# Spacing the first layer's attention steps in a woven program, charging gate loads to its issue clock, fetching gate rows ahead, and a later place for the first layer's block sums

## The chip, the core and the metric

The kernel runs on one core of a Trainium2 chip. Its time is device microseconds of that core, as the median of several runs. Five engines work side by side: TensorE (PE in the profile; PEld is its weight load), VectorE (DVE), ScalarE (ACT), GpSimd (POOL), and SyncE (SP), which here only issues DMAs. Each engine runs its own instructions in program order and waits on semaphores for the others.

## What is computed

Two layers of a trunk over 512 latent and 256 context tokens, 1024 channels wide. The reference, cut to what matters:

```python
for l in range(DEPTH):                       # DEPTH = 2
    sh, sc, gt = split(silu(c) @ w_ada[l] + b_ada[l])        # for latents; the same from c_ctx for the context
    h = rmsnorm(x, g_pre[l]) * (1 + sc) + sh
    p = split(h @ w_in[l])                   # columns for: conv, attention, GLA, SiLU paths, merge gates
    att = softmax_attention(q, k, v)         # 8 query heads, 2 key/value heads, rotary on latents
    gla = bidirectional_gla(q, k, v, decay)  # 4 heads, chunked linear attention
    br_a = (conv mixer * silu(z)) @ w_br_conv[l]
    br_b = (att * silu(z_attn)) @ w_br_attn[l]
    br_c = (rmsnorm(gla, g) * silu(z_gla)) @ w_br_gla[l]
    out = (g_a * br_a + g_b * br_b + g_c * br_c) @ w_out[l]
    x = x + gt * rmsnorm(out, g_post[l])     # the context stream too, in the first layer
```

## The kernel before

Every product is made in three passes of float32 parts: an operand is split into a high part (ACT copies, line 143) and a low part (DVE subtracts, line 134). Most DVE work goes through one helper, `tt` at line 134, so tiles and not lines tell its instructions apart.

The program is a hand-made list of steps. A `Step` (line 76) holds a function that emits instructions, the weight units it needs, a `cost` (its PE time in ns as the author counts it), and a `lat`, the latency that should lie in front of it. `weave(main, side)` (line 85) lays a list of dependent steps (side) into a list of independent products (main): it adds up `cost * room` over main, divides by the sum of `lat` over side, and lets each side step come as soon as main steps worth its `lat` times that scale have been placed.

In the first layer there are two weaves. The first (line 1634) lays `mods_next` into main: the next layer's modulation (`small_vectors`, two `ada_half`) and this layer's gate rows (`gate_rows`, line 507). The second (line 1640) lays attention and then the four GLA heads (`side = att + sum(heads, [])`) into main. Main there is, in this order: one convolution block, then 34 pairs of projections (`pair_steps`, line 335, seven steps p1 to p7 each; a pair shares work between two column blocks by sums of blocks), then the products of the convolution branch (`w_br_conv`) and of the attention branch (`w_br_attn`), four steps a column block. The 64 branch steps have `room = 1.7`, which makes them count for more main than they cost. Eight empty steps of cost 1500 and eight of 2500 (`behind`, line 1215) stand between them for loads of branch inputs; they bring no PE work.

The latencies come from a table; the first number of each pair is the first layer's:

```python
"kv_ctx": (2400, 1500), "kv": (1500, 1200), "k_rope": (1000, 2000), "k_rot": (2500, 2500), "k_tr": (4000, 4000),
"q_ctx": (2400, 1500), "q": (1500, 1500), "q_rope": (2500, 2500), "q_rot": (2500, 2500), "q_tr0": (5000, 5000),
"q_tr1": (1500, 1950), "values": (500, 500), "weights": (3000, 3000), "scores": (1000, 1500),
"g_r": (1920, 2400), "g_q": (1500, 1500), "g_parts": (0, 0), "g_decays": (1000, 1000), "g_k": (1500, 1500),
"g_decays2": (0, 300), "g_v": (1500, 1500), "g_v2": (1500, 1500), "g_diag": (1500, 1500), "g_lev0": (2500, 2500),
"g_lev": (5500, 5500), "g_fin": (1500, 562), "g_ktr": (5000, 5000), "g_qfin": (0, 800), "g_st0": (3000, 3000),
"g_st1": (1000, 500), "g_st2": (1000, 1600), "g_outtr": (1000, 1000), "g_scaled": (1000, 1000),
"g_outs": (1500, 1500),
```

Attention (line 566) has, for each of 2 key/value heads and 2 pairs of query heads, projections into PSUM, norms and rotation on ACT and DVE, transposes, and then six rounds of three steps: `scores` (line 699: PE at line 708 into the tile psA, maxima on DVE, exponentials on ACT), `weights` (line 723: normalisation on DVE at lines 752 and 753, transposes on PE at line 158 into psA, a split by ACT and DVE into pThi and pTlo) and `values` (PE, line 761). psA has two buffers, which scores, weights, the larger bursts of projections, and GLA share.

A GLA head (line 783) has projections q, k and v (`side_cols`, `v_burst`), `decays` (line 833), a `diagonal` and seven `level` steps (line 940: products on PE at line 899, then on DVE two merges into a, two products into Q, two into K, one masked copy into att, and two products on POOL), then `finals`, transposes (`key_tr`), `states` (line 975), `outs` (line 996), `scaled` (line 1012) and `out_tr` (line 1025).

`gate_rows(l)` computes the gate as eight small products into the tile `mod`, then one last step (line 509): for each of two rows (b_ada, to be added, and g_post, to be multiplied) it clears a tile gp on POOL, loads the row into it by two DMAs on SP, and applies it to `mod` on DVE, all in one step.

Ahead of the first weave, at the start of the first layer, the input is normalised, transposed and modulated in four quarters of two blocks of 128 channels (`first_h`, line 1523). Each quarter has four steps: `scaled` (DVE scales and shifts into x0T, ACT writes the high part of hT), `sums` (DVE forms sums and differences of blocks into t, which only the pairs need; not in the last quarter), `low` (DVE writes the low part of hT, which every product needs) and `parts` (ACT and DVE split t into tx). Lines 1612 to 1614 write out their order between the modulation's quarters and the steps C, X and Z of the first convolution block, whose matmuls (line 238, tiles psA<-hT,hl) read hT quarter by quarter.

The list is walked once at build time (lines 1691 to 1749) with an issue clock that adds up the steps' costs. `advance` decides at each step which weight unit is loaded next (if a buffer of its ring is free) and which is split next: not before the issue clock has passed the unit's assumed arrival, `dma + LOAD_NS`, where `dma` adds up the time of each unit loaded. Other loads, such as those of stored gates `sg` and of partial sums `m` in the branches (lines 1266, 1269 and 1327), do not enter `dma`.

Of the kernel before, what the change touches and what calls it, by code (L numbers as in the profile page):

```python
# [17 lines left out]
P = 128  # L18
D = 1024
# [81 lines left out]
def trunk(ctx, tc, T, out):  # L101
# [16 lines left out]
    def L(dt=F32, name="l"):  # L118
        return pool.tile([P, 512], dt, tag="L", bufs=3, name=name)
# [9 lines left out]

    mm, act, dve, pl = nc.tensor.matmul, nc.scalar, nc.vector, nc.gpsimd  # L130
    load = nc.sync.dma_start

    def tt(o, a, b, op, e=dve):
        e.tensor_tensor(out=o, in0=a, in1=b, op=op)  # L134
# [371 lines left out]

    def gate_rows(l):

        def fn():
            for src, op in ((T["b_ada"][l][2 * D:], ALU.add), (T["g_post"][l], ALU.mult)):  # L510
                t = L(name="gp")[64:128, :512]
                pl.memset(t, 0.0)
                for j in range(2):
                    load(out=t[32 * j:32 * j + 2, :], in_=src[j * 512:(j + 1) * 512].partition_broadcast(2))
                tt(mod[64:128, :], mod[64:128, :], t, op)

        return ada_rows(l, (2 * D, 2 * D + 512), (64,)) + [Step(fn, lat=3)]

    def gate_broadcast(gb, t, j):
        pb = psB()  # L520
# [724 lines left out]
    def branch(l, nq, br, wname, Y, vec, mg_dram, sg_d=None):  # L1245

        def src_y(kb, c):
            return [t[:, c] for t in Y[kb]]

        S = []  # L1250
        for nb in range(NK):
            c = {}
            rows = slice(nb * P, (nb + 1) * P)
            tile_of = M if sg_d is None else G

            def evac_g(ps, st, c=c, nb=nb):
                c["sg"] = M(name="sg")
                act.activation(out=c["sg"][:, :nq], in_=ps[0][1], func=AF.Sigmoid,
                               bias=vec["v"][:, V_GATE + br * 8 + nb:V_GATE + br * 8 + nb + 1])
                if br == 0:  # L1260
                    exp_table()

            def before(st, c=c, rows=rows, tile_of=tile_of):
                if sg_d is not None:
                    c["sg"] = M(name="sg")
                    load(out=c["sg"], in_=sg_d[rows, :])
                if br > 0:
                    st["m"] = tile_of(name="m")
                    load(out=st["m"][:, :nq], in_=mg_dram[br - 1][rows, :nq])

            def evac_y(ps, st, c=c, rows=rows):
                sg = c["sg"]
                for x, p in ps:
                    tt(sg[:, x], sg[:, x], p, ALU.mult)
                if br > 0:
                    tt(sg[:, :nq], sg[:, :nq], st["m"][:, :nq], ALU.add)
                later.append(lambda: load(out=mg_dram[br][rows, :nq], in_=sg[:, :nq]))

            if sg_d is None:
                S += col_steps(unit_a(T["w_in"][l], O_MG + br * D + nb * P), src_h, nq, evac_g)  # L1280
            S += col_steps(unit_a(T[wname][l], nb * P), src_y, nq, evac_y, before)
        return S

    def branch_c(l, nq, u_dram, vec, mg_dram, merged, sz, sg_d=None, z_d=None):
# [36 lines left out]
        for nb in range(NK):  # L1321
            def before(st, nb=nb):
                st["m"] = (M if z_d is None else G)(name="m")
                pl.dma_start(out=st["m"][:, :nq], in_=mg_dram[1][nb * P:(nb + 1) * P, :nq])
                if sg_d is not None:
                    sg[nb] = G(name="sg")
                    load(out=sg[nb], in_=sg_d[nb * P:(nb + 1) * P, :])

            def evac_y(ps, st, nb=nb):
                t = sg[nb]  # L1330
                for x, p in ps:
                    tt(t[:, x], t[:, x], p, ALU.mult)
                tt(st["m"][:, :nq], t[:, :nq], st["m"][:, :nq], ALU.add)
                merged.append(split_to(st["m"][:, :nq], nq))

            rest += col_steps(unit_a(T["w_br_gla"][l], nb * P), src_y, nq, evac_y, before)
# [254 lines left out]
    for l in range(DEPTH):  # L1591
# [15 lines left out]
        if l == 0:  # L1607
# [1 line left out]
            (q0, f0), (q1, f1), (q2, f2), (q3, f3) = quarters  # L1609
            split = lambda u: Step(lambda: None, u[0].units)  # L1610
            ctx_loads[-1].opens = C[0].units
            prog += q0 + [Step(lambda kb=kb: raw_h(kb)) for kb in range(4, NK)] + [f0] + h0[0][:1] + [split(C)] + h0[0][1:]
            prog += [C[0], split(X)] + q1 + [X[0], split(Z), f1] + h0[1] + [Z[0], C[1]] + q2 + [X[1], f2] + h0[2] + [Z[1], C[2]]
            prog += q3 + [X[2], f3] + h0[3] + [sv[1], Z[2], C[3], X[3], Z[3]]
            prog += [Step(lambda: set_masks(0, 4)), Step(lambda: set_masks(4, 7))]
        else:
            hs = lagged(h_steps(0, range(NK), vec))
# [10 lines left out]
        if l == 0:  # L1628
# [7 lines left out]
                s.cost = max(s.cost, 1.0)  # L1636
            for s in main[main.index(first[-32]):]:
                s.room = 1.7
            side = att + sum(heads, [])
            woven = weave(main, side)  # L1640

# [47 lines left out]
        return n  # L1689

    clock, settled, ends = 0.0, 0, []
    dma = 0.0

    def finish(u):

        if u.rest:
# [7 lines left out]

    def advance(i, needed):

        nonlocal n_load, n_prep, settled, dma
        for u in units[:n_load]:
            if u.rest and clock >= u.done + REST_NS:
                finish(u)  # L1710
# [4 lines left out]
        while moved:  # L1715
            moved = False
            if n_load < len(units) and live(i, units[n_load].ring) < AHEAD[units[n_load].ring] and i >= hold.get(id(units[n_load]), 0):
                u = units[n_load]
                u.load(u)
                dma = max(dma, clock) + u.ns  # L1720
                u.arrival = dma + LOAD_NS
                n_load += 1
                moved = True
            if n_prep < len(line) and line[n_prep] in units[:n_load]:
# [74 lines left out]
```

## Time and profile before

| | us |
|---|---|
| median of 3 runs | 2536.9 (2532.49, 2536.9, 2538.5) |
| the profiled execution's own time | 2529.78 |
| its span, first to last instruction | 2528.0 |
| DVE busy | 1493.9 (59%) |
| ACT busy | 976.7 (39%) |
| POOL busy | 306.6 (12%) |

The times in all that follows are microseconds from the start of the span. In a view of stretches, each row gives a stretch, its length, the busy time of PE, PEld, DVE, ACT and POOL in it with the number of instructions, the share of its clock that TensorE was granted, the busy share of the DMA engines and their GB/s. In a view of groups, a row gives line, engine, operation, tiles out<-in, shapes and count, then the busy time, the mean duration in ns, and the engine's idle time just before those instructions with what ended it. In the view of instructions in order of time, a row gives start, duration, engine, line, operation, tiles, count, and in brackets the idle time before it with what ended it.

In the first layer, attention's steps run from about 97 to 726 us and GLA's from 726 to 1364 us; the pairs of projections end near 1047 us, where the branch products begin. The layer's output product follows, and the second layer runs from about 1510 us.

### The profile page before, as it was taken

What the parts mean: (1) busy time and instruction counts of PE and PEld (TensorE: products, weight loads), DVE (VectorE), ACT (ScalarE), POOL (GpSimd) and SP (SyncE); (2) the same over time, 40 slices, a digit from 0 to 9 for tenths busy, and PEclk for the clock granted to TensorE, in tenths of its full rate; (3) what the DMA queues carried; (4) which work ended last, traced back from release to release, by engine and by line L of the source; (5) the groups of instructions that cost most, each with busy time, mean ns of one, the idle gap of its engine ahead of it and who ended that gap; (6) DMA issues with size and microseconds to landing.
All of it is one profiled execution on the core that took longest, in us unless ns stands there. A gap on an engine that the chain in (4) does not pass through costs nothing. (4 is left out here: it accounts for less than half of the span.)

```text
span 2528.0 us, 34629 instructions
## 1 busy us (share of the span) xinstructions
PE 2369.9 (94%) x13733; PEld 2134.4 (84%) x13733; DVE 1493.9 (59%) x2475; ACT 976.7 (39%) x1498; POOL 306.6 (12%) x375
## 2 busy tenths in 40 slices
PE   5998999899899999899798999999999999999998
PEld 3888988889789999889698978888888878888887
DVE  4566586786758668555455543664665456554554
ACT  3334443343434454431312243543545343424232
POOL 1100100100002011020111022011011111111100
PEclk8999999999999999999898999999999999999999
DMA  6322333213213333542445432222322333333333
GB/s 206 99 91 78 106 107 93 86 57 89 86 59 115 105 118 103 160 133 93 129 136 191 138 114 72 78 78 74 90 71 85 92 97 114 112 110 108 96 109 104
DMA packets 334127, 264.42 MB, mean 105 GB/s; under 512 B 18648, under 2 KB 294412, under 8 KB 333964
## 3 DMA queue, kind: packets, MB, share of 16 engines
q1 hardware_dynamic: 332252, 256.44, 33.1%
q0 software_dynamic: 1648, 5.75, 0.7%
q8 instruction: 108, 1.77, 0.3%
q14 instruction: 55, 0.45, 0.1%
q10 hardware_dynamic: 64, 0.02, 0.0%
HBM read 219.42 MB, written 42.73 MB: 104 GB/s over the span
## 5 line engine op out<-in xcount | busy, mean ns | idle before, releaser
L238 PE MATMUL psB<-hT,hl 128*128 128x512 f32 (+1 forms) x2400 | 560.8, 386 | 4.9 <-DVE y L1037 2.8
L238 PEld LDWEIGHTS psB<-hT,hl 128*128 128x128 f32 x2400 | 441.0, 190 | 81.0 <-issue 6.7
L134 DVE TENSOR_TENSOR hl<-raw,hl 128x1024 fp32r<-128x1024 f32 x292 | 367.4, 1270 | 158.4 <-ACT hl L143 156.2
L143 ACT CAST hl<-raw 128x1024 fp32r<-128x1024 f32 x292 | 300.8, 1046 | 276.8 <-PE psB L238 95.1
L353 PE MATMUL psB<-hT,hl 128*128 128x384 f32 x1734 | 327.9, 338 | 0.8 <-DVE cd L134 0.8
L353 PEld LDWEIGHTS psB<-hT,hl 128*128 128x128 f32 x1734 | 304.3, 189 | 3.9 <-issue 1.7
L245 PE MATMUL psA<-hl,hT 128*128 128x256 f32 x1968 | 240.1, 283 | 2.1 <-DVE hl L134 2.1
L245 PEld LDWEIGHTS psA<-hl,hT 128*128 128x128 f32 x1968 | 238.8, 192 | 3.9 <-DVE hl L134 2.6
L238 PE MATMUL psB<-hi,hl 128*128 128x384 f32 (+1 forms) x768 | 210.6, 367 | 0.0
L353 PE MATMUL psB<-tx,hl 128*128 128x384 f32 x918 | 189.6, 351 | 10.6 <-DVE hl L134 7.4
L353 PEld LDWEIGHTS psB<-tx,hl 128*128 128x128 f32 x918 | 165.1, 196 | 21.8 <-DVE hl L134 9.7
L238 PE MATMUL psA<-hT,hl 128*128 128x512 f32 x864 | 167.9, 353 | 16.3 <-DVE hT L134 7.8
L238 PEld LDWEIGHTS psA<-hT,hl 128*128 128x128 f32 x864 | 140.1, 194 | 43.1 <-DVE hT L134 9.3
L238 PEld LDWEIGHTS psB<-hi,hl 128*128 128x128 f32 x768 | 140.6, 191 | 15.5 <-issue 2.5
L134 POOL TENSOR_TENSOR rstd<-ms,mhalf 128x1 f32<-128x1 f32 (+4 forms) x54 | 54.4, 1007 | 787.2 <-DVE ms L167 605.0
L134 POOL TENSOR_TENSOR Sf<-Sf,a 128x384 f32<-128x384 f32 x56 | 62.4, 1113 | 503.7 <-DVE K L134 271.7
L238 PE MATMUL psB<-lo,hl 128*128 128x384 f32 (+1 forms) x384 | 117.1, 359 | 0.0
L134 DVE TENSOR_TENSOR sg<-sg,psB 128x384 f32<-128x384 f32 (+1 forms) x72 | 40.8, 594 | 106.6 <-PE psB L238 106.6
L720 ACT ACTIVATE pe<-psA,nmx 128x768 f32<-128x768 f32 (+1 forms) x80 | 65.1, 816 | 93.4 <-DVE nmx L711 86.1
L245 PE MATMUL psB<-hl,hT 128*128 128x256 f32 x720 | 89.8, 283 | 4.5 <-DVE hl L134 4.5
L134 DVE TENSOR_TENSOR pTlo<-psA,pThi 128x768 fp32r<-128x768 f32 (+1 forms) x72 | 64.2, 923 | 50.1 <-ACT pThi L138 49.9
L134 DVE TENSOR_TENSOR raw<-raw 128x384 f32<-128x384 f32 (+1 forms) x170 | 90.9, 551 | 4.8 <-DMA raw<-in_w_in 1.2
(275 smaller groups left out, 3530.8 us busy)
## 6 DMA issues: line engine op xcount, KB each, us to landing
raw<-in_w_in SPq DMA_DIRECT2D x192, 512.0 KB
raw<-in_w_ada SPq DMA_DIRECT2D x64, 256.0 KB
sg<-sp SPq DMA_DIRECT2D x24, 384.0 KB
raw<-in_w_br_conv SPq DMA_DIRECT2D x16, 512.0 KB
raw<-in_w_br_attn SPq DMA_DIRECT2D x16, 512.0 KB
raw<-in_w_br_gla SPq DMA_DIRECT2D x16, 512.0 KB
raw<-in_w_out SPq DMA_DIRECT2D x16, 512.0 KB
sp<-c SPq DMA_DIRECT2D x20, 384.0 KB
```

The lines of the kernel that those rows point to most:

```text
L134: e.tensor_tensor(out=o, in0=a, in1=b, op=op)
L143: act.copy(out=hi, in_=src)
L238: mm(p, lhsT=w[a][:, kb, :], rhs=src(kb, c)[s], start=(kb == 0 and i == 0), stop=(kb == NK - 1 and i == 2))
L245: mm(ps, lhsT=h_block(kb, tb, a), rhs=w[s][:, kb % 4, :], start=(kb == 0 and i == 0), stop=(kb == NK - 1 and i == 2))
L353: mm(ps, lhsT=w_[a], rhs=x[b], start=(j == 0 and z == 0), stop=(j == len(todo) - 1 and z == 2))
L720: act.activation(out=pe[:, k0:], in_=ps[:, k0:NT], func=AF.Exp, bias=nmx, scale=SCALE, accum_out=sm)
```

## The change

Four edits. In the first layer every attention step's `lat` is multiplied by 1.5 ahead of the second weave; GLA's are not. The loads of `sg` and `m` go through `big_load`, which adds 1100 ns to the issue clock's `dma` for each. The last step of `gate_rows` becomes four: fetch b_ada's row, (the last of the eight products), add it, fetch g_post's row, multiply by it; the tile gp moves from the ring L to the one buffer of the ring s1, which the pairs use for one of their operands. At the start of the first layer `low` now follows `scaled` at once, and `sums` and `parts` of each quarter come some products later, the last of them between the convolution block's fourth X step and its fourth Z step.

```diff
+    dma = [0.0]
+    def big_load(out, in_):
+        load(out=out, in_=in_)
+        dma[0] += 1100.0
...
     def gate_rows(l):
-        def fn():
-            for src, op in ((T["b_ada"][l][2 * D:], ALU.add), (T["g_post"][l], ALU.mult)):
-                t = L(name="gp")[64:128, :512]
-                pl.memset(t, 0.0)
-                for j in range(2):
-                    load(out=t[32 * j:32 * j + 2, :], in_=src[j * 512:(j + 1) * 512].partition_broadcast(2))
-                tt(mod[64:128, :], mod[64:128, :], t, op)
-        return ada_rows(l, (2 * D, 2 * D + 512), (64,)) + [Step(fn, lat=3)]
+        rows = []
+        def fetch(src):
+            t = pool.tile([P, NT], F32, tag="s1", bufs=1, name="gp")[64:128, :512]
+            pl.memset(t, 0.0)
+            for j in range(2):
+                load(out=t[32 * j:32 * j + 2, :], in_=src[j * 512:(j + 1) * 512].partition_broadcast(2))
+            rows.append(t)
+        def apply(op):
+            tt(mod[64:128, :], mod[64:128, :], rows.pop(0), op)
+        a, b = T["b_ada"][l][2 * D:], T["g_post"][l]
+        S = ada_rows(l, (2 * D, 2 * D + 512), (64,))
+        return S[:-1] + [Step(lambda: fetch(a), lat=1), S[-1], Step(lambda: apply(ALU.add), lat=2), Step(lambda: fetch(b), lat=1),
+                         Step(lambda: apply(ALU.mult), lat=2)]
...
             def before(st, c=c, rows=rows, tile_of=tile_of):
                 if sg_d is not None:
                     c["sg"] = M(name="sg")
-                    load(out=c["sg"], in_=sg_d[rows, :])
+                    big_load(out=c["sg"], in_=sg_d[rows, :])
                 if br > 0:
                     st["m"] = tile_of(name="m")
-                    load(out=st["m"][:, :nq], in_=mg_dram[br - 1][rows, :nq])
+                    big_load(out=st["m"][:, :nq], in_=mg_dram[br - 1][rows, :nq])
...
                     sg[nb] = G(name="sg")
-                    load(out=sg[nb], in_=sg_d[nb * P:(nb + 1) * P, :])
+                    big_load(out=sg[nb], in_=sg_d[nb * P:(nb + 1) * P, :])
...
-            prog += q0 + [Step(lambda kb=kb: raw_h(kb)) for kb in range(4, NK)] + [f0] + h0[0][:1] + [split(C)] + h0[0][1:]
-            prog += [C[0], split(X)] + q1 + [X[0], split(Z), f1] + h0[1] + [Z[0], C[1]] + q2 + [X[1], f2] + h0[2] + [Z[1], C[2]]
-            prog += q3 + [X[2], f3] + h0[3] + [sv[1], Z[2], C[3], X[3], Z[3]]
+            (a0, s0, l0, p0), (a1, s1, l1, p1), (a2, s2, l2, p2), (a3, s3, l3, p3) = h0
+            prog += q0 + [Step(lambda kb=kb: raw_h(kb)) for kb in range(4, NK)] + [f0, a0, split(C), l0]
+            prog += [C[0], split(X)] + q1 + [X[0], split(Z), f1, a1, l1, Z[0], C[1], s0] + q2 + [X[1], f2, a2, l2, p0, Z[1], C[2], s1]
+            prog += q3 + [X[2], f3, a3, l3, p1, sv[1], Z[2], s2, C[3], X[3], p2, s3, p3, Z[3]]
...
             for s in main[main.index(first[-32]):]:
                 s.room = 1.7
+            for s in att:
+                s.lat *= 1.5
             side = att + sum(heads, [])
             woven = weave(main, side)
...
-                dma = max(dma, clock) + u.ns
-                u.arrival = dma + LOAD_NS
+                dma[0] = max(dma[0], clock) + u.ns
+                u.arrival = dma[0] + LOAD_NS
```

More of the change, by code (lines that the diff above doesn't have):

```diff
@@ L1691, in trunk @@
     clock, settled, ends = 0.0, 0, []
-    dma = 0.0
     def finish(u):
@@ L1705, in advance @@
     def advance(i, needed):
-        nonlocal n_load, n_prep, settled, dma
+        nonlocal n_load, n_prep, settled
         for u in units[:n_load]:
```

## The prediction

> **What bounds the kernel now.** I read the page first, then PE's busy time by stretch, then PE's groups within the stretches that lose time, and last the order in time around single waits.
>
> ```profile
> PE 2369.9 (94%) x13733; PEld 2134.4 (84%) x13733; DVE 1493.9 (59%) x2475; ACT 976.7 (39%) x1498; POOL 306.6 (12%) x375
> ```
>
> PE sets the time: of 2528.0 us of span it is idle for 158. No edit changes its matmuls, so only its waits, and the slower clock that follows them, can be won or lost. By stretch:
>
> ```profile
> 37.00:82.00 45.00, 35.88 (x204) 24.87 (x205) 26.64 (x63) 11.52 (x20) 0.00 (x0) 0.85 0.32 100
> 126.00:726.00 600.00, 546.01 (x3432) 522.23 (x3431) 414.48 (x741) 249.75 (x402) 35.39 (x54) 0.96 0.29 87
> 726.00:1044.00 318.00, 313.37 (x1932) 296.93 (x1932) 224.01 (x366) 141.94 (x180) 37.78 (x38) 1.00 0.35 107
> 1044.00:1362.00 318.00, 286.03 (x1704) 269.17 (x1702) 176.46 (x280) 82.65 (x125) 48.06 (x54) 0.95 0.43 140
> 764.00:842.00 78.00, 77.69 (x484) 75.06 (x483) 70.64 (x113) 34.13 (x41) 15.84 (x15) 1.00 0.41 124
> 664.00:670.00 6.00, 5.45 (x26) 5.25 (x27) 3.89 (x8) 2.17 (x5) 0.00 (x0) 0.72 0.37 109
> ```
>
> PE's idle time is length less busy time: 9.1 us at the start, 54.0 in attention, 4.6 in GLA beside the pairs, 32.0 in GLA beside the branches. What the clock takes is length times one less the granted share: 6.8, 24, 0 and 16 us. So attention loses 78 us where GLA beside the same pairs loses 5: the main work is spread unevenly over the side steps. The last row shows that a short wait has a price beyond itself: it begins just after one of 1.4 us, and 0.28 of 6 us, 1.7 us, is lost to the clock.
>
> **Attention's spacing.** The table's latencies, first layer: a key/value head has 11,400 for its own projections, and twice 15,400 for a query pair's and six rounds of 500 + 3000 + 1000, so 96,200; two make 192,400. A GLA head has 66,000; four and g_r make 265,920. Main is worth 7,800 (convolution) + 34 pairs of 3 x 1557 + 4 x 2595 = 15,051 + 64 branch steps of 1950 x 1.7 + 46,000 (empty steps) + 9,600 (products of 600), together 787,300. Scale before: 787,300 / 458,320 = 1.718. After: 787,300 / (288,600 + 265,920) = 1.420. An attention step gets 1.5 x 1.420 / 1.718 = 1.24 times the main work, a GLA step 0.83 times. Attention ends 79,000 of main later.
>
> Which of attention's waits are waits for distance? The groups of PE in 126 to 726:
>
> ```profile
> L353 PE MATMUL psB<-tx,hl 128*128 128x384 f32 x554 | 117.1, 356 | 8.1 <-DVE hl L134 6.8 <-ACT hl L143 1.2
> L158 PE MATMUL psA<-ident,pe 128*128 128x128 f32 x224 | 31.4, 284 | 15.5 <-DVE rs L752 14.8
> L245 PE MATMUL psB<-hl,hT 128*128 128x256 f32 x240 | 30.1, 283 | 3.0 <-DVE hl L134 3.0
> L708 PE MATMUL psA<-kThi,qThi 128*128 128x256 f32 x48 | 14.9, 311 | 7.2 <-DVE pTlo L134 7.1
> L708 PE MATMUL psA<-kThi,qThi 128*128 128x512 f32 x32 | 14.3, 447 | 13.6 <-DVE pTlo L134 7.0 <-DVE qTlo L134 6.6
> PE psA L158 <- DVE rs L752: 14.8, 7, 4.2
> ```
>
> First, `weights` (line 158) waits seven times for the sums of the exponentials. Two rounds in order of time, scores' last matmuls and then the transposes:
>
> ```profile
> 496.11 0.51 PE L708 MATMUL psA<-kThi,qTlo 128*128 128x512 f32 x2
> ...
> 506.40 2.82 PE L158 MATMUL psA<-ident,pe 128*128 128x128 f32 x12 [4.25 <-DVE rs L752]
> ...
> 528.56 0.28 PE L708 MATMUL psA<-kThi,qTlo 128*128 128x256 f32 x1
> ...
> 537.63 0.60 PE L158 MATMUL psA<-ident,pe 128*128 128x128 f32 x4
> ```
>
> The first had two products of a pair in front and waited; the second had three and started without a wait. 3000 x 1.718 = 5154 of main comes to two or three products of 1557 or 2595, 3000 x 2.130 = 6390 to three nearly always. Laid out by `weave`, 13 of the 24 stand behind at most two products before, and two after; those two have products of 2595. I take 15.5 down to 1.5: 14.0 won. Bounds: 0, and 15.5.
>
> Second, `scores` (line 708) waits 20.8 us, mostly for pTlo, that is for one of psA's two buffers. 1000 x 1.718 and 1000 x 2.130 both come to one product, sometimes none: four stand right behind `weights` before, five after. I take 20.8 down to 13: 7.8 won, between 0 and 20.8. Third, 11.1 us for split weights, where DVE (414.48 of 600 us) is late; thinner side work lets it catch up: to 8, so 3.1 won. Of the other 6.5 us I take 1.4. Sum: 26.3 of 54.0 us.
>
> The clock's 24 us go by how many waits there are rather than how long they are. Some four in ten go: 10 us won, bounds 0 and 24. Attention: 36 us. By the Trainium skill (TensorE: Matmul & The Clock Gate, section What's actually happening) the clock halves only after an idle window of about 3.4 us; by that rule removing waits of 1 or 2 us would win no clock, and the sum would be 8 us smaller. The row of 664 to 670 speaks against it here.
>
> **GLA at 0.83 of its spacing.** Beside the pairs PE waits 4.6 us, but there DVE has little left: 70.64 of 78 us in the levels of the first head, where these are the level's own:
>
> ```profile
> L134 DVE TENSOR_TENSOR Q<-q,a 128x384 f32<-128x384 f32 x14 | 7.9, 596 | 0.4 <-ACT a L856 0.3
> L134 DVE TENSOR_TENSOR a<-a 128x384 f32<-128x384 f32 x14 | 7.1, 549 | 0.0
> L946 DVE COPY_PREDICATED att<-masks,psA 128x768 f32<-128x768 uint8 x6 | 6.2, 1036 | 0.0
> L134 DVE TENSOR_TENSOR K<-k,Pb 128x384 f32<-128x384 f32 x6 | 3.3, 550 | 0.0
> L134 DVE TENSOR_TENSOR K<-k,Sf 128x384 f32<-128x384 f32 x6 | 3.3, 550 | 0.0
> ```
>
> That is 27.8; the other 42.8 belong to pairs and shrink with the distance to 35.4, so DVE needs 63.2 us. PE's 77.7 hold seven levels of some 1.5 us; the rest shrinks to 55.5, so PE needs 66. DVE goes from 91% to 96%, not past PE. I take 5 us of waits for this in two heads, between 0 and 18. Beside the branches:
>
> ```profile
> L1007 PE MATMUL psA<-st,a 128*128 128x256 f32 x60 | 17.6, 407 | 6.7 <-DVE st L992 6.7
> L158 PE MATMUL psB<-ident,on 128*128 128x128 f32 x32 | 6.3, 318 | 10.3 <-DVE on L1016 10.3
> L899 PE MATMUL psA<-Q,k 128*128 128x128 f32 x24 | 4.4, 353 | 2.7 <-DVE Q L134 2.7
> L158 PE MATMUL psA<-ident,Sf 128*128 128x128 f32 x18 | 2.5, 274 | 1.7 <-DVE Sf L134 1.7
> L838 PE MATMUL psA<-rT,wd 96*128 96x512 f32 x4 | 1.7, 448 | 3.3 <-DVE wd L134 3.3
> ```
>
> After the change the third head's levels 4 to 6, and its `key_tr`, `states` and `outs`, fall among the eight empty steps of 2500, which cover nothing. I price: those levels 5 (one product between them, where DVE's 4 us a level and the branch's own exceed it); three steps with nothing in front 1.7 each, 5; `decays` with nothing in front four times instead of twice, 1.65 each, 6.6; first levels with one product in front, half of 2.7 each, 4; last `out_tr` of three heads 1.5 each, 4.5; the last head's end as now, 4.4; `outs` behind a load 4. With the 5 above 38.5, where the two stretches have 36.6 now: 2 us lost, clock unchanged. Bounds 20 won, 41 lost (below).
>
> **Gate rows.** The old step holds DVE in its queue while it waits for its own two loads, and `out_tr` behind it:
>
> ```profile
> L134 DVE TENSOR_TENSOR mod<-mod,gp 64x512 f32<-64x512 f32 x2 | 1.4, 689 | 6.5 <-DMA gp<-in_b_ada 4.1 <-DMA gp<-in_g_post 2.3
> L158 PE MATMUL psB<-ident,on 128*128 128x128 f32 x8 | 2.5, 445 | 10.0 <-DVE on L1016 10.0
> POOL gp L512 <- DVE mod L134: 3.5, 1, 3.5
>   DMA gp<-in_b_ada: 6.1, 2
> ```
>
> Those 10.0 us of PE are in the 10.3 above, which I have let go but for the 4.5 of `out_tr`; the gain of this edit stands in that sum. `mods_next` wants 64 instead of 61, and its weave is worth 637,000, so the first row is applied 4/64 of it, 40 us of products, after its fetch and the second 20 us after: the 4.1 us are hidden. Two clears, four loads and two DVE operations stay. The fetch's clear waits on POOL for the pairs' last reading of s1, and behind it stand GLA's merges on POOL and, on SP, the four loads and the weights; the old clear waited 3.5 us too, so 0, between 3.5 lost and 3.5 won. In the second layer DVE waits the remaining 2.0 of 6.1 us, off PE's path: 0.
>
> **Loads in the issue clock.** No instruction is added; 40 loads of 1100 ns let a unit's split be emitted later. The 6.7 us at line 1007 are such a split, stuck on ACT for a load, with DVE's states behind it; the 4 above takes 2.7 off. Bounds: 6.7 either way, since a split emitted late keeps PE waiting for hl.
>
> **The start.** PE's groups in 37 to 82 (three quarters with `sums`) and 82 to 100 (the last, without), and DVE in the first:
>
> ```profile
> L238 PE MATMUL psA<-hT,hl 128*128 128x512 f32 x36 | 17.1, 499 | 12.3 <-DVE hT L134 7.4 <-ACT hl L143 4.3 <-ACT hT L1532 0.6
> L238 PE MATMUL psA<-hT,hl 128*128 128x512 f32 x12 | 4.5, 416 | 0.7 <-DVE hT L134 0.4 <-ACT hT L1532 0.3
> 39.20 1.02 DVE L134 TENSOR_TENSOR t<-x0T 128x384 f32<-128x384 f32 x2
> 40.14 1.14 DVE L134 TENSOR_TENSOR t<-x0T,t 128x384 f32<-128x384 f32 x2
> 41.20 1.82 DVE L134 TENSOR_TENSOR hT<-x0T,hT 128x768 fp32r<-128x768 f32 x2
> ```
>
> `sums` stands 2.0 us ahead of the low part. Three times that is 6.0 of the 7.4; half of the clock's 6.8 goes with it, 3: 9 us won, between 6 and 12. The moved steps fit on DVE, busy 26.64 of 45 us.
>
> **The sum** is 36 - 2 + 9 = 43 us: the profiled execution's 2529.8 becomes 2486.8, and the median of 2536.9, 7.1 above it, becomes 2494.
>
> **The rivals.**
> *Only `weights` gains* (0.20): psA's two buffers and DVE stay late whatever the distance. For it: 14 of scores' 20.8 us are for pTlo; against it: the calm of 726 to 1044. Attention wins 14 + 6 of clock, the start 9, GLA loses 9 (its DVE near the bound of 18): 20 us, 2517. The Trainium skill (Perfetto Trace Analysis, section Optimization Strategy) reads gaps that repeat as a possible shortage of PSUM for the next tile; the wait for pTlo agrees, with its 14 us.
> *Slower* (0.10): GLA is too close. Some 16 steps then have nothing in front of them; at 3.7 us each (a quarter of the 14.7 that four `out_tr` waits cost: the 10.3 and the last head's 4.4) they make 59, with half as much again for the clock (16 beside 32.0) 89, where 48 are now: 41 lost against 22 in attention and 9 at the start: 2547. It decides where the mean wait passes 3.3 us.
> *The clock stays* (0.08): waits get shorter but not fewer; 26.3 + 6 - 2 + 2 won, 2505, the rule of the clock gate above.
> *More* (0.10): attention comes as near as GLA to no waits: 10 us idle and 6 of clock left, 62 won, 8 beside the branches, 9 at the start: 2458.
> *It moves steps and nothing else* (0.05): splits forced by need and products of fixed size leave the waits as many: 2537.
>
> **How the numbers follow.** The forecast has 0.47. The range reaches from between *more* and the forecast to nothing gained, 2466 to 2537, and leaves out *slower* and part of *more*. 0.3%, 7.6 us, is about what a measurement can tell: faster by that 0.79 (forecast, *more*, clock, most of the first rival), the same 0.10, slower 0.11.
>
> **What would show it.** Right: line 158's wait for rs near zero in attention, PE's idle time there near 28 of some 650 us with a clock of 0.98; hT at the start near 1.4; no wait for gp on DVE; the pairs ending nearer to attention's end. Wrong: L708's wait for pTlo at 20 us or more, L899 waiting for Q or K in the third head's levels, DVE full beside the first head's levels with PE waiting for hl.

## The result, and the profile after

| | before | after |
|---|---|---|
| median, us | 2536.27 | 2500.52 |
| runs, us | 2532.49 to 2538.5 (4) | 2495.04, 2496.89, 2504.15, 2507.71 |
| the profiled execution's own time, us | 2529.78 | 2504.15 |
| its span, us | 2528.0 | 2502.4 |

The ratio of after to before is 0.9862 [0.9831, 0.9894]: 36 us faster, inside the range and beside the forecast of 2494. But the profiled execution of before lies 6.5 us under its median, that of after 3.6 us above, so the two profiles are only 25.6 us apart, where the forecast's sum, made against the profile, had 43. The mechanism has to be checked against the 25.6.

Where each stage ends is read from the last start of a line's instructions. These are rows of the view of one line, with duration (min/median/max, ns), then first and last start: attention's first weight loads, its last values, the last pair, the last out_tr. Before:

```profile
L245 PEld LDWEIGHTS psB<-hl,hT x64: 186/192/192, 96.9 to 130.0; 128*128 128x128 f32 x64
L761 PE MATMUL psB<-pThi,vlo x112: 279/283/415, 201.8 to 725.2; 128*128 128x256 f32 x112
L158 PE MATMUL psB<-ident,on x48: 270/273/476, 901.8 to 1363.4; 128*128 128x128 f32 x48
```

After (lines lie 6 or 13 further down):

```profile
L251 PEld LDWEIGHTS psB<-hl,hT x93: 186/192/192, 88.9 to 129.9; 128*128 128x128 f32 x93
L774 PE MATMUL psB<-pThi,vlo x112: 274/283/288, 205.6 to 790.4; 128*128 128x256 f32 x112
L359 PE MATMUL psB<-hT,hl x1734: 331/334/526, 98.2 to 1013.5; 128*128 128x384 f32 x193
L164 PE MATMUL psB<-ident,on x48: 270/273/473, 953.3 to 1343.3; 128*128 128x128 f32 x48
```

The start is 8.0 us shorter (96.9 to 88.9). From there to the last out_tr, the whole woven program, it was 1266.5 us and is 1254.4: 12.1 won, where the forecast had 34. Between these two starts PE's idle time fell by 13.1 us (91.2 to 78.1) and its busy time rose by 1.0 (1175.3 to 1176.3). The rest, 1164.6 and 1159.1 us, won 5.5 that nobody forecast. Attention ends 65 us later, and the pairs end 223 us behind it, no longer 322 (their last start was at 1047.0 us before).

The page's line of busy time of after comes first (PE is idle for 137 us of the span, where it was 158; of the 25.6 us between the profiles, 20.9 are idle time and 4.7 busy time), and then the busy time by stretch: the start, attention, GLA beside the pairs, GLA beside the branches, and the first head's levels:

```profile
PE 2365.2 (95%) x13733; PEld 2129.4 (85%) x13733; DVE 1493.5 (60%) x2475; ACT 974.5 (39%) x1497; POOL 307.9 (12%) x375
```

```profile
37.00:75.00 38.00, 34.47 (x210) 24.37 (x211) 22.05 (x53) 8.02 (x13) 0.00 (x0) 0.91 0.38 119
118.00:790.00 672.00, 626.77 (x3912) 602.27 (x3912) 472.52 (x843) 292.14 (x454) 38.28 (x54) 0.97 0.32 94
790.00:1014.00 224.00, 215.60 (x1285) 198.02 (x1284) 145.28 (x236) 95.17 (x125) 28.80 (x28) 0.99 0.33 100
1014.00:1344.00 330.00, 306.34 (x1885) 289.24 (x1885) 197.98 (x312) 86.79 (x130) 55.11 (x64) 0.97 0.43 138
835.00:894.00 59.00, 58.11 (x352) 55.30 (x353) 55.27 (x93) 23.76 (x29) 13.03 (x13) 1.00 0.28 82
```

PE's idle time in attention went from 54.0 to 45.2 us, not to 28. GLA's two stretches went from 36.6 to 32.1 us, the start from 9.1 to 3.5. The last row is the place where the prediction feared DVE: DVE is busy for 55.27 of 59 us, 94%, and PE is idle for 0.9 us there. PE's groups in attention after:

```profile
L359 PE MATMUL psB<-tx,hl 128*128 128x384 f32 x702 | 141.4, 346 | 9.7 <-DVE hl L140 9.7
L164 PE MATMUL psA<-ident,pe 128*128 128x128 f32 x224 | 28.6, 273 | 2.6 <-DVE rs L765 2.5
L251 PE MATMUL psB<-hl,hT 128*128 128x256 f32 x240 | 32.9, 299 | 5.1 <-DVE hl L140 5.1
L721 PE MATMUL psA<-kThi,qThi 128*128 128x256 f32 x48 | 15.1, 315 | 4.9 <-DVE pTlo L140 4.9
L721 PE MATMUL psA<-kThi,qThi 128*128 128x512 f32 x32 | 16.0, 501 | 19.4 <-DVE pTlo L140 15.6 <-DVE qTlo L140 3.5
```

and from the view of waits there (us in total, times, longest) the one that matters:

```profile
PE psA L721 <- DVE pTlo L140: 20.5, 16, 3.0
```

The wait of `weights` is gone (15.5 to 2.6), as forecast. But `scores` waits 24.3 us where it waited 20.8, and the split weights 14.8 where it was 11.1.

### The profile page after: what moved, and what is told of

It reads as the page before. It is cut to its first block, busy times and chain, and to the rows that moved or that the text cites. A ratio compares the mean times of both kernels' runs of the same rounds, so it can differ in the third digit from the quotient of the medians.

```text
span 2502.4 us, 34620 instructions
## 1 busy us (share of the span) xinstructions
PE 2365.2 (95%) x13733; PEld 2129.4 (85%) x13733; DVE 1493.5 (60%) x2475; ACT 974.5 (39%) x1497; POOL 307.9 (12%) x375
## 5 line engine op out<-in xcount | busy, mean ns | idle before, releaser
L140 DVE TENSOR_TENSOR hl<-raw,hl 128x1024 fp32r<-128x1024 f32 x292 | 362.0, 1254 | 153.3 <-ACT hl L149 151.0
L359 PE MATMUL psB<-tx,hl 128*128 128x384 f32 x918 | 185.7, 346 | 10.6 <-DVE hl L140 10.6
L359 PEld LDWEIGHTS psB<-tx,hl 128*128 128x128 f32 x918 | 162.4, 193 | 17.9 <-DVE hl L140 12.4
L251 PEld LDWEIGHTS psB<-hl,hT 128*128 128x128 f32 x720 | 92.3, 199 | 8.0 <-DVE hl L140 7.4
```

What stands on the lines that cost most here:

```text
L251: mm(ps, lhsT=h_block(kb, tb, a), rhs=w[s][:, kb % 4, :], start=(kb == 0 and i == 0), stop=(kb == NK - 1 and i == 2))
L359: mm(ps, lhsT=w_[a], rhs=x[b], start=(j == 0 and z == 0), stop=(j == len(todo) - 1 and z == 2))
```

## The experiments

Times are medians, ratios are to the kernel before on the same chip (its medians there were 2533.2 to 2534.0). Parts first, then the waits.

**The factor alone**, in the kernel before:

```diff
+            for s in att:
+                s.lat *= 1.5
             side = att + sum(heads, [])
```

> The kernel before with attention's latencies times 1.5 and nothing else. Theory (waits handed on): weights' wait for rs falls from 14.8 us in attention to about 3, but scores' waits for pTlo stay near 20, so attention gains some 9 us with the clock, GLA 3 at most, and the gate rows' 10 us wait of PE stays: about 2524 us. Rival (the prediction's sum: distance helps scores and hl as well, 36 us in attention): 2505 us or less. Second rival (the gain lies in the other three edits): 2536 us.

Measured: 2503.25 us, 0.9882 [0.9869, 0.9894], 30.7 us faster: the rival's 2505, not the theory's 2524. Nearly the whole change is this edit. PE's waits in attention (total, times, longest):

```profile
PE psA L708 <- DVE pTlo L134: 15.6, 11, 3.9
PE psA L158 <- DVE rs L752: 4.8, 5, 2.5
```

As in the changed kernel, weights' wait falls, by 10 us, and scores' does not: so the rival's time came without the gain at scores that it rests on. Of the span's 28.2 us (2528.0 to 2499.8), 17.6 are idle time of PE (158.1 to 140.5), 11.5 of them in attention (54.0 to 42.5). The other 10.6 are PE's busy time for the same matmuls (2369.9 to 2359.3), while the granted clock of the span went from 0.977 to 0.983.

**All but the factor**, the changed kernel without those two lines:

```diff
-            for s in att:
-                s.lat *= 1.5
```

> The changed kernel without the factor 1.5. Theory: the start's 8 us and the gate rows' 10 us and some of the loads' 3 us are still won: about 2516 us, with weights' wait for rs in attention back near 15 us. Rival (the spacing brings nearly all): 2530 us. The gains of this run and of the factor alone should add up to the 36 us of the whole change if the parts don't touch one another.

Measured: 2531.36 us, 0.9991 [0.9981, 1.0002]: no difference. The rival's number, and the 2.6 and 30.7 us add up to 33 of the 36. But it says that the other three edits bring nothing together, so they follow one by one.

**The start's new order alone**, in the kernel before:

```diff
+            (a0, s0, l0, p0), (a1, s1, l1, p1), (a2, s2, l2, p2), (a3, s3, l3, p3) = h0
-            prog += q0 + [...] + [f0] + h0[0][:1] + [split(C)] + h0[0][1:]
+            prog += q0 + [...] + [f0, a0, split(C), l0]
...
```

> The kernel before with the new order of the first-layer start only. Theory: the convolution block ends 8 us earlier and the rest is as before: about 2528 us; PE's wait for hT at the start near 1 us where it was 7.4. Rival (the gain is given back, since sums and parts now fall among the last convolution steps and attention's first bursts): 2536 us.

Measured: 2521.61 us, 0.9956 [0.9943, 0.9969], 12.4 us faster, 4 more than the theory's 8; where those 4 come from is not shown. The first three quarters' products in this kernel:

```profile
L238 PE MATMUL psA<-hT,hl 128*128 128x512 f32 x36 | 15.6, 463 | 6.7 <-ACT hl L143 4.3 <-DVE hT L134 1.9 <-ACT hT L1532 0.6
```

DVE's hT costs 1.9 us instead of 7.4; what is left, 4.3, is the split of weights. The stretch 37 to 75 has a clock of 0.91, as in the changed kernel, where 37 to 82 had 0.85.

**The gate rows alone**, in the kernel before:

```diff
-        return ada_rows(l, (2 * D, 2 * D + 512), (64,)) + [Step(fn, lat=3)]
+        return S[:-1] + [Step(lambda: fetch(a), lat=1), S[-1], Step(lambda: apply(ALU.add), lat=2), Step(lambda: fetch(b), lat=1),
+                         Step(lambda: apply(ALU.mult), lat=2)]
...
```

> The kernel before with the four-step gate rows only. Theory: DVE no longer waits for gp, but the next instruction in its queue waits for zg, whose load lands at the same time as before, so PE's two out_tr gaps stay: within 3 us of the kernel before, or slower, as the three edits without the spacing came to 2.6 us won where the start alone won 12.4. Rival (the prediction's term: the 10.0 us at out_tr go): 10 us or more faster than before.

Measured: 2533.68 us, 1.0013 [0.9998, 1.0028]. The theory holds, the 10 us do not come: PE's waits at `out_tr` over all four heads come to 15.4 us, where they were 14.7. Why they stay is read in DVE's instructions in order of time, at the place of the prediction's 10.0 us. Before:

```profile
1209.76 0.69 DVE L134 TENSOR_TENSOR mod<-mod,gp 64x512 f32<-64x512 f32 x1 [4.14 <-DMA gp<-in_b_ada]
1212.80 0.69 DVE L134 TENSOR_TENSOR mod<-mod,gp 64x512 f32<-64x512 f32 x1 [2.35 <-DMA gp<-in_g_post]
1213.52 0.88 DVE L1037 SCALAR_TENSOR_TENSOR on<-psB,vec,zg 128x256 f32<-128x256 f32 x2
```

The kernel of all but the factor, where the rows are fetched ahead and the same GLA head stands at the same time:

```profile
1208.80 0.69 DVE L140 TENSOR_TENSOR mod<-mod,gp 64x512 f32<-64x512 f32 x1
1214.17 0.88 DVE L1050 SCALAR_TENSOR_TENSOR on<-psB,vec,zg 128x256 f32<-128x256 f32 x2 [4.68 <-DMA zg<-sp]
```

`mod` no longer waits, and `on` starts at 1214.17 instead of 1213.52, since now zg holds it. zg's load was issued at 1208.37 here, 5.8 us before, and at 1205.23 in the kernel before: with the same 5.8 us, an estimate, `on` could have started there at 1211.0, so gp's wait cost it some 2.5 us, and the rest stood in front of zg's. With the gate rows alone, DVE waits 23.1 us for zg in all, six times; in the kernel before it was 16.9, six times too. The edit also has a price elsewhere: beside the pairs (722 to 1064 us) PE is idle for 16.0 us with the gate rows alone, where it was 4.6, with waits for the products' tile `mod` (3.1), for `on` (3.5) and for split weights (8.8) among them.

**The loads in the issue clock alone**, in the kernel before (three such places):

```diff
-                    load(out=c["sg"], in_=sg_d[rows, :])
+                    big_load(out=c["sg"], in_=sg_d[rows, :])
```

> The kernel before with the loads of sg and m in the issue clock only. Theory: splits are emitted later and PE sometimes waits for hl, which costs about as much as it saves: within 4 us of the kernel before. Rival (the prediction's term): 2.7 us faster, not told from the first at this resolution. Second rival (this edit is what the other two lose, some 10 us): 8 us or more slower than before, with PE's waits for hl in the branches 5 us or more above before.

Measured: 2530.87 us, 0.9996 [0.998, 1.0011]. No difference. The wait that it should shorten:

```profile
L1013 PE MATMUL psA<-st,a 128*128 128x256 f32 x60 | 17.6, 407 | 6.2 <-DVE st L998 6.2
```

6.7 became 6.2: half a microsecond, where 2.7 was forecast.

**The factor and the start together**, in the kernel before, without gate rows and loads:

```diff
-            prog += q0 + [...] + [f0] + h0[0][:1] + [split(C)] + h0[0][1:]
+            prog += q0 + [...] + [f0, a0, split(C), l0]
...
+            for s in att:
+                s.lat *= 1.5
```

> The changed kernel with gate rows and loads as before: the factor 1.5 and the new start alone. Theory (alone they won 30.7 and 12.4 us, and touch different stretches): 43 us won, 2490 us, so the gate rows and the loads in the issue clock take 8 to 10 us back in the changed kernel. Rival (the start's 12 us are given back by attention's spacing, whatever the gate rows do): 2500 us, as the changed kernel.

Measured: 2496.13 us (2493.58 to 2501.43), 0.9852 [0.9825, 0.988]: between the theory's 2490 and the rival's 2500, and its interval overlaps that of the changed kernel, 0.9862 [0.9831, 0.9894]. These two edits are the change; the other two bring nothing that can be measured. The start is worth 12.4 us alone and 7.1 on top of the factor. Without the factor the gate rows and the loads take the start's gain back (2521.61 with the start alone, 2531.36 with all three). One place is visible: in the kernel of all but the factor, GLA beside the pairs has

```profile
715.00:1055.00 340.00, 323.31 (x1960) 304.10 (x1959) 229.80 (x372) 143.08 (x182) 38.70 (x39) 0.98 0.34 105
```

16.7 us of PE idle, where the kernel with the start alone has 5.3 (715 to 1039). Of the two edits it is the gate rows that bring this: alone they have 16.0 us there (above), the loads alone 5.1 (726 to 1044). `gate_rows` has 64 parts instead of 61 in the first weave, and every product behind moves by a little; that this shift is the reason is likely but not shown. With the gate rows alone the time as a whole did not rise, so the idle time there is part of the answer at most.

**Scores further apart.** The changed kernel with one number changed:

```diff
-"values": (500, 500), "weights": (3000, 3000), "scores": (1000, 1500),
+"values": (500, 500), "weights": (3000, 3000), "scores": (2000, 1500),
```

> The changed kernel with the first layer's latency of scores 2000 in place of 1000 in the table (3000 after the factor 1.5), so that two products stand between weights and scores. Theory (a wait that weights no longer has lets DVE stay behind, and scores then finds psA unread): scores' wait for pTlo falls from 20.5 us to 7 or less, and with the clock some 15 us are won against the changed kernel: about 2485 us. Rival (DVE is late whatever the distance): the wait turns into others, for hl or rs, and the time stays at 2500 us within 4. Second rival (GLA, now at 0.94 of the spacing that it has in the changed kernel, loses more than scores gains): 2505 us or more.

Measured: 2476.73 us (2472.4 to 2477.36), 0.9772 [0.9759, 0.9785], 24 us faster than the changed kernel. The scale is now 787,300 / 590,520 = 1.333, so scores stands 3000 x 1.333 = 4000 of main behind weights instead of 2130, by the products' costs two of them and no longer one. The stretch of attention, and then PE's waits in it:

```profile
118.00:782.00 664.00, 638.34 (x4038) 616.09 (x4037) 486.51 (x869) 301.67 (x464) 38.23 (x54) 0.98 0.33 99
```

```profile
PE psA L164 <- DVE rs L765: 6.9, 3, 4.7
PE psB L359 <- DVE hl L140: 5.9, 2, 5.1
PE psA L721 <- DVE pTlo L140: 4.1, 5, 1.6
```

20.5 us at scores became 4.1, and PE's idle time in attention 25.7: the prediction's 28 is reached, by an edit that the change did not have. The theory's reason is another matter. It had DVE behind with its work. In the changed kernel's longest such wait, PE, then ACT, then DVE, in order of time:

```profile
750.45 1.47 PE L164 MATMUL psA<-ident,pe 128*128 128x128 f32 x12
751.67 2.86 PE L359 MATMUL psB<-hT,hl 128*128 128x384 f32 x15
757.49 0.78 PE L721 MATMUL psA<-kThi,qThi 128*128 128x512 f32 x1 [2.96 <-DVE pTlo L140]
```

```profile
751.18 1.28 ACT L1205 ACT_TABLE_LOAD   x1
752.48 0.94 ACT L1205 ACTIVATE e<-cd,vec 128x768 f32<-128x768 f32 x1
753.32 0.92 ACT L1206 ACTIVATE c<-c,vec 128x768 f32<-128x768 f32 x1
754.26 1.28 ACT L182 ACT_TABLE_LOAD   x1
755.55 0.20 ACT L182 ACTIVATE tiny<-one 128x1 f32<-128x1 f32 x1
755.66 1.48 ACT L144 CAST pThi<-psA 128x768 fp32r<-128x768 f32 x2
```

```profile
756.48 1.82 DVE L140 TENSOR_TENSOR pTlo<-psA,pThi 128x768 fp32r<-128x768 f32 x2 [5.78 <-ACT pThi L144]
```

DVE has been idle for 5.78 us. ACT is late: a pair ended just then, and ACT changes its function table, runs two activations, changes back (1.28 us each way) and only then evicts the transposes: weights ended at 751.92, pThi starts at 755.66. The wait is put down to DVE's pTlo because that came last. So DVE's backlog falls as the general reason, but the table changes are not the general one either. Of the 16 waits, five (9.1 of 20.5 us) have a table change on ACT between the transposes and pThi; in four (5.4 us) DVE did other work after pThi was ready, as the theory had it; the other seven (6.0 us) show neither at that place. That the evictions come late for one product, and that the wait goes with two, is shown.

**Scores further apart without the factor**, in the kernel before:

```diff
-"values": (500, 500), "weights": (3000, 3000), "scores": (1000, 1500),
+"values": (500, 500), "weights": (3000, 3000), "scores": (3000, 1500),
```

> The kernel before with the first layer's latency of scores 3000 in place of 1000 in the table, no factor 1.5 and none of the other edits. The scale becomes 1.555, so scores stands 4665 of main behind weights where it stood 1718, weights 4665 where it stood 5154. Theory (two waits with a distance each): scores' wait for pTlo falls from 14.0 us to under 5, weights' wait for rs stays at 15 us or rises to 20, so some 15 to 20 us are won: about 2517 us. Rival (DVE has one backlog and the wait only moves between the two): weights' wait grows by what scores' loses, within 5 us of the kernel before. Second rival (the distance of scores is all that matters): 2500 us or less.

Measured: 2528.19 us, 0.9983 [0.9972, 0.9995]: 5 us, less than the theory's 15 to 20, at the edge of the rival's bound of 5. Waits in attention:

```profile
PE psA L158 <- DVE rs L752: 17.4, 9, 3.8
PE psB L353 <- DVE hl L134: 12.6, 4, 4.3
PE psB L245 <- DVE hl L134: 5.1, 2, 2.7
```

No wait for pTlo is left at scores (14.0 before), but rs rose from 14.8 to 17.4 and hl from 9.8 to 17.7. So with the factor left out, most of the removed wait stands elsewhere. The same 3000 of scores (2000 x 1.5) with the factor won 24 us; there weights kept 4500 x 1.333 = 6000 of main, here it has 4665.

**The transposes into psB.** The changed kernel with weights' tiles in psB's four buffers, two blocks each, at the old distances.

```diff
-                    for i0 in range(0, len(blocks), 3):
-                        pt = psA()
+                    step = 2 if l == 0 else 3
+                    for i0 in range(0, len(blocks), step):
+                        pt = psB() if l == 0 else psA()
...
```

> The changed kernel with the first layer's transposes in weights written to tiles of psB, two blocks at a time in place of three, instead of psA; all distances as in the changed kernel. Six tiles of 512 columns take the place of four of 768 in a round over all keys, so ACT and DVE have one or two evictions more. Theory (scores waits for psA's two buffers, which weights' late evictions hold): PE's wait at scores for pTlo, 20.5 us, goes to under 3 without any more distance; some of it comes back at psB, which the pairs and values use: 5 to 12 us faster than the changed kernel, a ratio to the kernel before of about 0.982. Rival (DVE is late, and PE waits for it wherever the evictions write): scores' wait goes, but the pairs and values wait as much at psB: a ratio of 0.986 or more.

Measured: 2517.28 us, 0.9934 [0.9913, 0.9954], some 18 us slower than the changed kernel by the ratios. Groups in attention:

```profile
L164 PE MATMUL psB<-ident,pe 128*128 128x128 f32 x224 | 34.0, 293 | 14.0 <-DVE pe L767 6.4 <-DVE c L140 3.8 <-DVE cd L140 3.3
L359 PE MATMUL psB<-tx,hl 128*128 128x384 f32 x702 | 142.5, 347 | 18.2 <-DVE hl L140 10.3 <-DVE c L140 5.7 <-DVE uo L140 1.4
```

Scores' wait for pTlo is gone altogether, and the waits are at psB: the rival, and worse. The pairs, which write psB too, wait 18.2 us where they waited 9.7. The run also has six smaller evictions where there were four, and what those cost by themselves was not measured. By the Trainium skill (Perfetto Trace Analysis, section Optimization Strategy) repeating gaps can mean too little PSUM. The row of scores' 20.5 us agrees that PE stood for a buffer; but buffers taken from psB moved the gaps and lengthened them, where distance removed most of them.

**The rotation in two steps**, on top of scores further apart: ACT's copies, and 2250 of latency later DVE's products (for the keys as for the queries):

```diff
                 S.append(Step(lambda Q=Q, nt=nt: rotate(Q, "q", nt, 2), lat=slack("q_rot")))
+                S.append(Step(lambda Q=Q, nt=nt: turn(Q, "q", nt), lat=1500 if l == 0 else 0))
...
```

> The kernel with scores further apart, and in the first layer attention's rotation cut into two steps, ACT's scaled copies and, 1500 of latency later (2250 after the factor 1.5), DVE's products. Theory (DVE, in order, stands at the rotation for ACT's copies with the splits of the weights behind it; one such place cost 7.0 us of PE): the pairs' excess in attention of 21 us falls to 12 and its clock loss with it, 8 to 12 us faster than with scores further apart alone: about 2467 us. Rival (the rotation's own work on DVE, some 5 us a head, is what delays the splits, not its wait): no change, 2477 us within 3.

Measured: 2483.48 us, 0.9816 [0.9792, 0.984], 11 us slower than without by the ratios: a miss. The wait that it aimed at, for hl, shrank from 5.9 us (longest 5.1) to 3.9 (longest 2.1), but weights' grew from 6.9:

```profile
PE psA L164 <- DVE rs L771: 9.5, 5, 3.5
```

**zg a step earlier**, on top of scores further apart: its load moves from `scaled` into `outs`:

```diff
-            def outs(cp, Hd=Hd, v_of=v_of):
+            def outs(cp, Hd=Hd, v_of=v_of, h=h):
+                if z_d is not None:
+                    Hd["z", cp] = L(name="zg")
+                    load(out=Hd["z", cp].rearrange("p (j t) -> p j t", j=2), in_=...)
...
```

> The kernel with scores further apart, and in GLA the load of zg (the stored gate of the output) issued in the step outs, one step ahead of scaled, from the same ring L. Theory (what holds out_tr in the first layer is zg's landing): DVE's wait for zg falls from 16.6 us to under 5, out_tr's excess in the first layer from 11 us to 5, and the wait for zg at the layer's end, some 5 us, goes too: 8 to 15 us faster than with scores further apart alone, about 2465 us. Rival (the ring L of three buffers, or the store ahead of it on SP, holds the load back wherever it is issued): no change, 2477 us within 3. Second rival (the earlier load takes a buffer from on, and scaled waits): slower.

Measured: 2469.32 us (2467.46 to 2470.92), 0.9761 [0.9738, 0.9783]; 7.4 us less than without by the medians, though the intervals overlap. DVE's wait for zg, 16.6 us, is gone, but out_tr within GLA waits as before, and the gain lies in the 20 us after the layer's GLA. First those 20 us, with scores further apart and then with zg early, then PE's wait at out_tr within GLA in the same two kernels:

```profile
1312.00:1332.00 20.00, 16.65 (x75) 16.36 (x74) 4.92 (x7) 2.51 (x3) 1.08 (x2) 0.77 0.57 210
```

```profile
1310.00:1330.00 20.00, 20.00 (x112) 20.00 (x111) 8.30 (x12) 3.35 (x4) 1.16 (x3) 0.95 0.52 198
```

```profile
PE psB L164 <- DVE on L1029: 9.1, 3, 4.2
```

```profile
PE psB L164 <- DVE on L1034: 9.4, 3, 4.4
```

So zg was one more wait in front of another: within GLA, out_tr waits for `on` with zg in time as well. That too few products stand between `scaled` and it is a guess that no run tried. The theory holds for the end and falls for the heads.

**uo a step earlier**, on top of that: its load moves from `weights` into `scores`:

```diff
                 def scores(n, Q=Q, K=K, h0=h0):
+                    n["U"] = L(name="uo")
+                    if z_d is not None:
+                        h = h0 + n["j"]
...
+                        load(out=n["U"][:, 256:], in_=z_d[h * P:(h + 1) * P, tp * 256:(tp + 1) * 256])
...
```

> The kernel with scores further apart and zg loaded a step earlier, and in attention the load of uo (the stored gate of a head) issued in scores, one step ahead of weights. Theory (DVE stands in its queue for uo with the splits of weights behind it): DVE's wait for uo falls from 6.6 us to under 1 and the one place where PE waits 5.1 us for hl goes: 4 to 7 us faster than without it, about 2464 us. Rival (DVE has the time, or the load then stands ahead of weights' loads on SP): 2469 us within 3.

Measured: 2469.12 us, 0.9747 [0.9725, 0.977]: the rival. DVE's wait for uo, 6.6 us, is gone, and PE's wait for hl is what it was, 5.9 us with a longest of 5.1.

The fastest kernels are these two, 64 us under the kernel before and some 30 under the changed one.

## Why the prediction was right, and where not

**Weights: right.** 14.0 us forecast; 15.5 went to 2.6.

**Scores: wrong, and this is the step that failed.** The prediction found that 1718 and 2130 of main "both come to one product, sometimes none", which is a reason for no gain, and still took 20.8 down to 13. It became 24.3. Its own sign of failure, a wait for pTlo of 20 us or more, came true with 20.5. Two products, not one, cover the evictions: with two in between, 20.5 us for pTlo became 4.1. Why one product went with more waiting than before, and not the same, is not shown.

**Split weights: wrong in sign.** 3.1 us won were forecast, 3.7 were lost (11.1 to 14.8). Together attention's idle time fell by 8.8 us, not 26.3.

**The clock: wrong in size, the rule about right.** The prediction let the loss follow the number of waits. The view of waits counts 36 of them in attention before, 31 after and 18 with scores further apart. What the clock itself did is seen when the row of 664 to 670 is cut finer, in the kernel before:

```profile
662.30:665.70 3.40, 1.75 (x13) 1.31 (x12) 3.30 (x5) 2.61 (x5) 0.00 (x0) 0.99 0.73 209
665.70:669.10 3.40, 3.40 (x14) 3.40 (x12) 2.13 (x4) 1.10 (x4) 0.00 (x0) 0.50 0.33 106
669.10:672.50 3.40, 3.40 (x26) 3.40 (x26) 1.51 (x7) 0.00 (x0) 0.00 (x0) 1.00 0.03 10
```

The traces' clock is either 1 or 0.5, and 0.5 comes in pieces of 3.41 us or of several times that. In the middle row PE is busy throughout with 14 matmuls, in the next one with 26. Each piece in attention began right behind 3.41 us in which PE was busy for at most 52%; the shortest wait that brought one was 1.41 us, the one above. There were ten pieces before, nine after and four with scores further apart, and by the shares 21.6, 20.5 and 10.2 us lost. So the edit removed one piece, about 1 us by the share, where 10 us were forecast: the waits that went were not those that bring a piece, or others took their place. Nor is the share's loss all time: a piece can fall where PE waits anyway. PE's busy time in the weave did not fall (1175.3 and 1176.3 us), so in the 12.1 us won there no gain of the clock is to be seen.

By the Trainium skill (TensorE: Matmul & The Clock Gate, section What's actually happening) PE drops to half its clock after an idle window of about 3.4 us. The traces agree with the half and with the 3.4 us; they do not bear out that PE must be idle for all of the window, since half of it was enough. The prediction gives the price of that rule as 8 us in its sum and as 11 in its rival (2494 to 2505); the second takes the start's 3 us of clock with it.

**GLA: the sum nearly right, the terms not.** 2 us lost were forecast; 4.5 of idle time were won. By the share the clock won 4 more (16 to 2.2 + 9.9), but no busy time (above). In the branch stretch after:

```profile
L912 PE MATMUL psA<-Q,K 128*128 128x128 f32 x203 | 26.0, 278 | 7.2 <-DVE K L140 7.1
L1020 PE MATMUL psA<-st,a 128*128 128x256 f32 x60 | 16.4, 382 | 0.9 <-DVE st L1005 0.8
L164 PE MATMUL psB<-ident,on 128*128 128x128 f32 x36 | 7.4, 318 | 10.4 <-DVE on L1029 10.3
L851 PE MATMUL psA<-rT,wd 96*128 96x512 f32 x4 | 1.8, 470 | 3.3 <-DVE wd L140 3.3
```

The levels wait 7.2 us (5 and 4 forecast); `decays` 3.3 here and 3.4 in the stretch before it (6.6 forecast); `outs` 0.9 (4 forecast). `out_tr` with the last head's end went from 10.3 + 4.4 to 10.4; the forecast had 4.5 + 4.4.

**Gate rows: wrong.** DVE no longer waits for gp in the first layer, but alone the edit won nothing: behind gp's wait stood zg's, and PE's waits at out_tr stayed (14.7 and 15.4 us). The prediction looked at what the instruction waited for, not at what the next one in the queue needed. It also had no price for the products that the four steps move: 11 us more of idle time beside the pairs.

**Loads: wrong in size.** 2.7 us forecast; the wait fell by 0.5 alone, and the time showed no difference.

**The start: right.** 9 us forecast; 8.0 in the profiles, 12.4 alone and 7.1 on top of the factor in the runs. The wait for hT fell from 7.4 to 1.9, with 1.4 forecast.

**Why the number came out well: in good part by luck.** In the profiles 25.6 us were won, where 43 were forecast: nearer to the rival *only weights gains*, which had 20. Its reason, that psA and DVE stay late "whatever the distance", is what the changed kernel shows and what the experiment with scores refutes. The medians lie 36 us apart: before's profiled execution lies under its median and after's above. And of the 25.6, 5.5 came from behind the weave, which the forecast had at nothing (in the 20 us after the last out_tr PE idles 2.9 us at a clock of 0.71 before, 1.4 at 0.90 after). The forecast of 2494 stands beside 2500.5 with one term of 7.8 us on the wrong side, 10 us of clock in attention of which no more than 1 came, a gain of the gate rows that did not come, and some 10 us between profile and median that nothing here explains. What held is the direction, the place of the largest gain (weights' wait, by the factor) and the start.

## What to carry to other kernels

When a latency is scaled, turn it into whole products: the distance that came to one product before and after bought nothing here, and its wait became the largest. Before pricing a removed wait at its full length, ask what else the same instruction and the one behind it in the queue need, and when that lands: gp's wait hid zg's, and zg's hid that of `on`. Buffers from another ring did not replace distance here, where the evictions themselves were late.

## What the runs showed of the hardware

A change of ACT's function table took 1.28 us here (38 times in attention after the change, a pair's end bringing two), and the activation after it started at once, 754.26 + 1.28 against 755.55. In the wait of 2.96 us the cost to PE came through the evictions queued behind two of them.

TensorE's granted clock was 1 or 0.5, never between, and 0.5 came in pieces of 3.41 us or several times that, behind a stretch of that length in which PE was busy for about half of it or less. Waits of 1.4 to 2.4 us were enough where they fell into one such stretch. A mean share such as 0.96 is a count of such pieces.

Executions of the changed kernel differ by 12.7 us (2495.04 to 2507.71), with the granted clock of the whole run between 0.981 and 0.985; a difference of two profiles can be off by as much.
